# Finishing a modulation block: sums over partitions with the accumulator streamed, copied and turned

## The chip, the cores and the metric

The kernel runs on one core of a Trainium2 chip. The metric is device time in microseconds (us) of one execution; the time of a kernel is the median over its runs. TensorE (PE) multiplies; loading its stationary operand ("weights") is a separate instruction and is shown as PEld. VectorE is DVE, ScalarE is ACT, GpSimd is POOL; SP starts most of the DMA transfers. Each engine works through its own instructions in order.

## The reference, cut to what matters

```python
for layer in range(DEPTH):                                   # DEPTH = 2, D_MODEL = 1024
    mod_x = split(s_c  @ w_mod[layer] + b_mod[layer], 6)     # one row for the latent tokens
    mod_c = split(s_cc @ w_mod[layer] + b_mod[layer], 6)     # one row for the context tokens
    hx = modulate(rms_norm(x,   norm_mix_g[layer]), mod_x[0], mod_x[1])
    hc = modulate(rms_norm(ctx, norm_mix_g[layer]), mod_c[0], mod_c[1])
    ...                                                      # mixer of the layer
    x = x + mod_x[2] * ox
    fx = modulate(rms_norm(x, norm_ffn_g[layer]), mod_x[3], mod_x[4])
    x = x + mod_x[5] * conv_ffn(fx, ...)
```

`s_c` and `s_cc` are SiLU of the two conditioning vectors. `w_mod[layer]` is 1024 x 6144 in float32. Layer 0 has a Mamba-2 SSD mixer and RG-LRU blocks, layer 1 has HGRN2 and S5; each layer ends in a convolutional feed-forward network (FFN). There are 512 latent and 256 context tokens.

## The kernel before

Activations lie with channels on partitions, in a tile of 768 columns (256 context, 512 latent). A matmul of full precision is three matmuls of rounded parts: line 215 sends, for each slice of 128 input channels, `whi` with the high part, `whi` with the low part and `wlo` with the high part, for 512 latent columns (tile `px`) and for 256 context columns (tile `pc`). ACT rounds each weight panel to `whi`, DVE makes the rest `wlo`; four buffers of each are in turn.

The modulation matrix is cut into blocks of 256 output columns, named (layer l, block j), 24 to a layer. The first eight blocks of layer 0 are made at the start with matmuls (`mod_cols`, line 308: four groups of 32 weight columns side by side in the array, each with its own input rows, then a copy by ACT and two transposes, line 316). Block (0, 21) has a way of its own (`mod_now`). The other 39 blocks are spread over the kernel as ticks:

- `mod_tick` (line 347) handles one slice of 128 input channels of a block: a 128 x 256 piece of `w_mod` comes by DMA into `mst` (two buffers), and DVE adds piece times `sc` (the conditioning, one value to a partition) to the accumulator `macc`. For 23 blocks (15 of layer 0 and the first 8 of layer 1) there are two accumulators, latent and context (n = 2); for the last 16 blocks of layer 1 there is one (n = 1).
- After 8 ticks `macc` holds, on each partition, a partial sum for 256 outputs. `mod_pend` (line 367) puts the block on the list `PEND`; each call of `mtick` lets every pending block take one stage. Two empty stages (LAG = 2) come ahead of `finish` (line 369).
- `finish` adds up over the 128 partitions: for each half h and each accumulator e a matmul on line 373 with the 128 x 128 half of `macc` as weights and one column of ones streamed, into one column of the PSUM tile `pmodt`. Then two DVE operations (line 375) add the bias and write `MOD`.
- `macc()` (line 268) gives the next block one of two accumulator buffers, and forces the oldest pending block on while more than one would be held.
- PSUM tiles named `pmodt`, and many others (`pin`, `pst`, `pyi`, `pcbm`, `pyt`, `pnst`, ...), come from one ring of three banks (`pss`, line 92): a tile waits until the tile three before it in the ring has been read.

The order of instructions on each engine is not the order of the code: a list scheduler sets it when the kernel is built, so an added instruction can move its neighbours. In layer 0's mixer (about 215 to 585 us) the LRU phase and the SSD phase are woven together; in the output projection of layer 0 (about 585 to 705 us) matmuls on `rhi`/`rlo` are woven with the last SSD steps: `pin` (line 1111), `pst` (line 1099), `pyt` (line 1201). The FFN of layer 0 follows.

Of the kernel before, what the change touches and what calls it, by code (L numbers as in the profile page):

```python
# [9 lines left out]
F32 = mybir.dt.float32  # L10
# [28 lines left out]
PNS = {}  # L39
# [25 lines left out]
def build(tc, I, out, dbg=None):  # L65
# [26 lines left out]
    def pss(name="ps"):  # L92
        return pp.tile([128, 512], F32, tag="ps", name=name, bufs=3)
# [109 lines left out]
    def wpanel(W, r0, kt, c0, n, gain=None, byk=False, eng=None):  # L203
        return wsplit(wload(W, r0, kt, c0, n), kt, n, gain, byk, eng)
# [33 lines left out]
    def mod_advance(q):  # L238

        q["stages"].pop(0)()  # L240
        if not q["stages"]:
            PEND.remove(q)
# [24 lines left out]

    def macc():

        while len(PEND) + (TICK[0] % NQ > 0) > 1:  # L270
            mod_advance(PEND[0])
        return mp.tile([128, 2 if LIM[0] < len(MODSEQ) else 1, 256], F32, tag="macc", name="macc", bufs=2)

    def mod_row(ps, r):
        row = macc()[:, 0]
        V.tensor_copy(row[:r], ps[:r, :256])
        return row

    def mod_split(l, j, eng=None):

        w = wpanel(I["w_mod"][l], 0, 8, j * 256, 256, byk=True, eng=eng)
        ps = pss("pmod")
        for k in range(8):
            hi, lo = w[k // 4]
            PE.matmul(ps[:4, :256], sc4[:, k, :], hi[:, k % 4, :], start=(k == 0), stop=False)
            PE.matmul(ps[:4, :256], sc4[:, k, :], lo[:, k % 4, :], start=False, stop=(k == 7))
        row = mod_row(ps, 4)
        PEND.append({"l": l, "j": j, "stages": [lambda: mod_finish(l, j, row, 2, 2)]})

    def mod_now(l, j, st=None):  # L290

# [32 lines left out]
    NQ = 8  # L324
# [1 line left out]
    MST = []  # L326
    MACC = []

    PE_ = [j for j in range(8, 20) if (0, j) in MODP]

    def mod_pe(at):

        if at in PNS and PE_:
            k = PNS[at]
            (mod_now(0, PE_.pop(0)) if k == 1 else mod_split(0, PE_.pop(0), G if k == 2 else V))

    def mod_load():
        i = len(MST)
        if i < NQ * LIM[0]:
# [26 lines left out]

    def mod_pend(l, j, n, acc, lag):

        def finish():
            pt = pss("pmodt")  # L370
            for h_ in range(2):
                for e in range(n):
                    PE.matmul(pt[:, 2 * h_ + e:2 * h_ + e + 1], acc[:, e, h_ * 128:(h_ + 1) * 128], ones[:, 0:1], start=True, stop=True)  # L373
            for h_ in range(2):
                V.tensor_scalar(MOD[l][j // 4][:, j % 4 * 2 + h_, 0:n], pt[:, 2 * h_:2 * h_ + n], P("bm", l * 48 + j * 2 + h_), None, op0=ALU.add)
        PEND.append({"l": l, "j": j, "stages": [lambda: None] * lag + [finish]})

    def mod_vec(l, j, st):

# [167 lines left out]
    J0 = [(i % 2 == 0) * 4 + i // 2 for i in range(8)]  # L547
    xin, ST0 = [], {}
    sc = cp.tile([128, 8, 2], F32, name="sc")
    sc4 = cp.tile([128, 8, 4], F32R, name="sc4")  # L550
    sc32 = ldp.tile([128, 8, 32], F32, name="sc32")
    G.memset(sc32, 0.0)
    par0 = fetch_par(0, ldp, S)
# [5 lines left out]
    def mod0(i):  # L559
        if START[i] == 1:  # L560
            mod_cols(0, J0[i], ST0.pop(i))
        elif START[i] == 3:
            mod_vec(0, J0[i], ST0.pop(i))
        else:
            mod_split(0, J0[i], G if START[i] == 2 else V)

    def xturn(c):
        for hf in range(2):
# [18 lines left out]
    for c in range(6):  # L587
        xturn(c)
        if c == LP0:

            turn_par(*par0)
            act(sc[:, :, 0], PS("c", 0, 8), AF.Silu)
            act(sc[:, :, 1], PS("cc", 0, 8), AF.Silu)
            V.tensor_copy(sc32[:, :, 0:2], sc)
            V.tensor_copy(sc4[:, :, 0:2], sc)
            V.tensor_sub(sc4[:, :, 2:4], sc, sc4[:, :, 0:2].bitcast(F32))
        if c in M0C and m0 < n1:
            mod0(m0)
            m0 += 1
# [122 lines left out]
    def xbc_phase(xp):  # L722

        dtg = dt_phase(xp)

        XI = [0]

        def turn(b, t):
            q0, q1 = pss("ptx"), pss("ptc")
            tk = xp.tile([128, 6, 128], F32, tag="tk", name="tk")  # L730
            for c in range(6):
                d_ = q1[:, c * 128:(c + 1) * 128] if c < 2 else q0[:, (c - 2) * 128:(c - 1) * 128]
                PE.transpose(d_, t[:, c * 128:(c + 1) * 128], ident)
            act(tk[:, 0:2, :], q1[:, :256].rearrange("p (c x) -> p c x", x=128), AF.Copy)
            act(tk[:, 2:6, :], q0.rearrange("p (c x) -> p c x", x=128), AF.Copy)
            if b < 8:
                S.dma_start(xtok_d[:, :, b * 128:(b + 1) * 128].rearrange("c p x -> p c x"), tk)
            else:
                S.dma_start(btok_d[:, :, (b - 8) * 128:(b - 7) * 128].rearrange("c p x -> p c x"), tk)

        prev = None
        for pb in (4, 5, 0, 1, 2, 3):
            w = wx4 if pb == 4 else wpanel(W0, 0, 8, 1024 + pb * 256, 256, eng=G if KG[7] else V)
            blk = []
            if pb == 4:
                blk = [(psx(), psc()) for hf in range(2)]
                mm3g([(both(*blk[hf]), w, hf) for hf in range(2)], h, range(8))
            for hf in range(2):
                b = pb * 2 + hf
                if pb == 4:  # L750
                    px, pc = blk[hf]
                else:
                    px, pc = psx(), psc()
                    mm3(both(px, pc), w, hf, h, range(8))
                t = xp.tile([128, T], F32, tag="t768", name="xbct", bufs=3)
                conv1d(t, px, pc, lambda i: P("scw", i * 12 + b), P("scb", b), 4,
                       xp.tile([128, T], F32, tag="ctap", name="ctap", bufs=1) if b in CVP else None)
                act(t, t, AF.Silu)
                dump(f"xbc_{b}", t)
                if b >= 10:  # L760
                    S.dma_start(cch_d[b - 10], t)
                elif b >= 8:
                    S.dma_start(bch_d[b - 8], t)
                yield
                mod_pe(XI[0] // 2)
                mtick(MT[0] if XI[0] >= SSD0 - 4 else MT[4])
                XI[0] += 2
                if b == 8 or (b == 9 and next(dtg, None)):
                    pass
                if prev is not None:  # L770
                    turn(*prev)
                prev = (b, t) if b < 10 else None
                yield
            next(dtg, None)
        turn(*prev)
        for _ in dtg:
            pass
# [582 lines left out]
    with tc.tile_pool(name="lru", bufs=2, reuse_waits="tile") as lp:  # L1360

        acc = 0.0
        for at, _ in enumerate(lru_phase(lp)):
            mod_pe(12 + at)
            mtick(MT[1])
            acc += SSDR
            if acc >= 1.0:
                acc -= 1.0
                if ssd is not None and next(ssd) == "gate":
                    acc = -1e9  # L1370
        while acc > -1e8 and next(ssd) != "gate":
            pass
# [769 lines left out]
```

## Time and profile before

| what | value |
|---|---|
| runs | 2121.35 us median of 3 (2115.91 to 2133.28) |
| the profiled execution | 2126.28 us, span 2124.4 us, mean granted clock 0.968 |
| PE busy | 2011.8 us, 95% |
| DVE busy | 1568.3 us, 74% |
| ACT busy | 870.1 us, 41% |
| matmul records of line 373 | 248, two to each of 124 matmuls |
| mean granted clock, 215 to 700 us | 0.94 |
| mean granted clock, 700 to 1330 us | 1.00 |

A float32 matmul leaves two records (the 124 matmuls of line 373 leave 248), a transpose one. A timeline row merges records of one kind that follow each other: "x8" are eight records, the first number is the start of the first, the second the time they covered. A row's length is latency, and matmuls are pipelined: what a matmul costs a busy TensorE is the distance from its start to the start of the next. The granted clock is given as a share of full speed; it has two levels, 1.2 and 2.4 GHz.

### The profile page before, as it was taken

How to read it: one execution, taken by the hardware profiler on the slowest of the kernel's cores; microseconds unless marked ns; L12 is line 12 of the kernel's file. 1: busy time of each engine (PE TensorE's matmuls, PEld its weight loads, DVE VectorE, ACT ScalarE, POOL GpSimd, SP SyncE). 2: the span in 40 equal slices, each digit the busy share in tenths (PEclk: the TensorE clock that was granted, in tenths of full speed). 3: DMA queues.
4: the chain of work that ended last, by engine and by line, in shares of the span. 5: the costliest groups of instructions: out<-in, count | busy, mean ns of one | idle time of the engine just before them, and what ended most of it. 6: DMA issues, size and time to landing. Idle time of an engine off the chain costs nothing.

```text
span 2124.4 us, 32677 instructions
## 1 busy us (share of the span) xinstructions
PE 2011.8 (95%) x12738; PEld 1696.7 (80%) x12738; DVE 1568.3 (74%) x2934; ACT 870.1 (41%) x1267; POOL 259.8 (12%) x223
## 2 busy tenths in 40 slices
PE   7969989898898999999999999999999899999998
PEld 4758778787677888888888888987888688888887
DVE  5998898767778888867775665655877779668484
ACT  4725576586533442212321223424444344223234
POOL 2132333344421000000000000120001000000000
PEclk7979999999899999999999999999999999999999
DMA  9437435435676322333234212454422123322321
GB/s 334 133 104 207 152 98 169 128 97 162 222 245 218 100 85 97 110 119 119 90 112 134 82 47 98 130 155 149 136 80 68 41 80 99 100 88 92 99 85 55
DMA packets 283018, 261.09 MB, mean 123 GB/s; under 512 B 23405, under 2 KB 263060, under 8 KB 282864
## 3 DMA queue, kind: packets, MB, share of 16 engines
q1 hardware_dynamic: 257504, 243.35, 36.1%
q10 hardware_dynamic: 24464, 13.75, 2.3%
q8 instruction: 100, 1.64, 0.3%
q0 software_dynamic: 896, 1.90, 0.2%
q14 instruction: 54, 0.44, 0.1%
HBM read 224.17 MB, written 34.78 MB: 122 GB/s over the span
## 4 chain that ended last, share of the span: by engine, by line
PE 64%; DVE 5%; DMA 3%; issue 1%; ACT 1%; POOL 1%; SPq 0%; DVEq 0%; POOLq 0%; ACTq 0%
PE px L215 34%; PE pc L215 10%; PE pu L215 6%; PE pseg L215 4%; DMA mst<-in_w_mod_dram 1%; DVE macc L83 1%; PE pmodt L373 1%; PE pv L222 1%; PE pv L223 1%; PE pv L224 1%; PE pob L215 1%; PE plv L1886 1%; DVE qx L1937 0%; PE py L1735 0%; DMA st<-in_ev_w_out_dram 0%
## 5 line engine op out<-in xcount | busy, mean ns | idle before, releaser
L80 ACT ACTIVATE whi<-st 128x1024 fp32r<-128x1024 f32 (+1 forms) x197 | 203.5, 1037 | 581.0 <-PE pc L215 372.8
L215 PE MATMUL px<-HH,whi 128*128 128x512 f32 (+2 forms) x1016 | 408.6, 404 | 9.8 <-DVE u L83 4.7
L215 PE MATMUL px<-HL,whi 128*128 128x512 f32 (+2 forms) x1016 | 404.9, 399 | 0.9 <-DVE HL L83 0.9
L215 PE MATMUL px<-HH,wlo 128*128 128x512 f32 (+2 forms) x1016 | 404.7, 398 | 0.0
L193 DVE TENSOR_TENSOR wlo<-st,whi 128x1024 fp32r<-128x1024 f32 (+1 forms) x197 | 237.3, 1208 | 78.6 <-ACT whi L80 76.5
L83 DVE SCALAR_TENSOR_TENSOR macc<-mst,sc,macc 128x256 f32<-128x256 f32 x434 | 216.0, 528 | 70.5 <-DMA mst<-in_w_mod_dram 69.8
L83 DVE SCALAR_TENSOR_TENSOR fa<-px,par,fa 128x441 f32<-128x441 f32 (+2 forms) x352 | 241.8, 692 | 8.1 <-ACT fa L80 2.0
L215 PEld LDWEIGHTS px<-HH,whi 128*128 128x128 f32 (+1 forms) x1016 | 191.9, 189 | 55.3 <-DVE u L83 5.2
L215 PEld LDWEIGHTS px<-HL,whi 128*128 128x128 f32 (+1 forms) x1016 | 192.3, 189 | 45.2 <-DVE HL L83 1.9
L215 PEld LDWEIGHTS px<-HH,wlo 128*128 128x128 f32 (+1 forms) x1016 | 192.0, 189 | 44.4 <-issue 0.4
L215 PE MATMUL pc<-HH,whi 128*128 128x256 f32 (+1 forms) x728 | 207.4, 287 | 10.0 <-ACT ge L80 4.7
L215 PE MATMUL pc<-HH,wlo 128*128 128x256 f32 x728 | 206.8, 285 | 0.0
L215 PE MATMUL pc<-HL,whi 128*128 128x256 f32 (+1 forms) x728 | 206.8, 285 | 0.0
L215 PEld LDWEIGHTS pc<-HH,whi 128*128 128x128 f32 (+1 forms) x728 | 138.3, 190 | 14.4 <-ACT ge L80 5.5
L80 ACT ACT_TABLE_LOAD x105 | 134.7, 1283 | 11.4 <-DVE fa L83 3.6
L215 PEld LDWEIGHTS pc<-HL,whi 128*128 128x128 f32 (+1 forms) x728 | 138.4, 190 | 1.2
L215 PEld LDWEIGHTS pc<-HH,wlo 128*128 128x128 f32 x728 | 138.0, 190 | 0.6
L215 PE MATMUL px<-fhi,whi 128*128 128x512 f32 x304 | 120.6, 397 | 0.0
L215 PE MATMUL px<-flo,whi 128*128 128x512 f32 x304 | 120.0, 395 | 0.0
L215 PE MATMUL px<-fhi,wlo 128*128 128x512 f32 x304 | 119.8, 394 | 0.0
L1843 POOL TENSOR_TENSOR kc<-kc,e 128x255 f32<-128x255 f32 x6 | 6.5, 1082 | 847.0 <-ACT kc L80 674.8
L215 PE MATMUL pu<-HH,wlo 128*128 128x512 f32 (+1 forms) x192 | 74.3, 387 | 0.0
(655 smaller groups left out, 4260.2 us busy)
## 6 DMA issues: line engine op xcount, KB each, us to landing
mst<-in_w_mod_dram SPq DMA_DIRECT2D x312, 128.0 KB, 2.1
st<-in_ffn_w_gate_dram SPq DMA_DIRECT2D x22, 1024.0 KB, 4.9
st<-in_ffn_w_up_dram SPq DMA_DIRECT2D x22, 1024.0 KB, 5.0
st<-in_ev_w_in_dram SPq DMA_DIRECT2D x18, 1024.0 KB, 6.3
st<-in_ffn_w_down_dram SPq DMA_DIRECT2D x16, 1024.0 KB, 4.9
bc<-cum_d SPq DMA_DIRECT2D x24, 512.0 KB, 6.0
sth<-in_od_w_in_dram SPq DMA_DIRECT2D x24, 512.0 KB, 4.1
st<-in_w_mod_dram SPq DMA_DIRECT2D x9, 1024.0 KB, 11.2
```

What stands on the lines that cost most here:

```text
L80: return S.activation(o, i, f, bias=bias, scale=scale, **kw)
L83: return (eng or V).scalar_tensor_tensor(o, a, s, b, op0=op0, op1=op1)
L193: (eng or V).tensor_sub(lo, src, hi.bitcast(F32))
L215: PE.matmul(o, ww[:, k, :M], hh[k][part][:, sl], start=(first and q == 0 and a == 0), stop=(stop and q == last and a == 2))
L222: PE.matmul(o, hh[k][0][:, sl], whi[:, k % 4, :], start=(k == 0), stop=False)
L223: PE.matmul(o, hh[k][0][:, sl], wlo[:, k % 4, :], start=False, stop=False)
L224: PE.matmul(o, hh[k][1][:, sl], whi[:, k % 4, :], start=False, stop=(k == 7))
L373: PE.matmul(pt[:, 2 * h_ + e:2 * h_ + e + 1], acc[:, e, h_ * 128:(h_ + 1) * 128], ones[:, 0:1], start=True, stop=True)
L1843: G.tensor_mul(kc[:, 0, 0:255], kc[:, 0, 0:255], e0[:, 0:255])
L1886: PE.matmul(v3[r:r + 32, c, :], kk(j), qq(j), start=True, stop=True, tile_position=(0, r))
```

## The change

The ones become the weights and the accumulator is streamed. Each block's end is now two stages and not one. `sums`: for each of the 2n halves a matmul with 32 columns of ones as weights, in one of four column groups of the array (`tile_position=(0, q * 32)`), with 128 columns of `macc` streamed, so that every one of the 32 partitions of a group in the PSUM tile `pmods` holds the sums; then ACT copies the 128 x 128 (n = 2) or 64 x 128 (n = 1) tile to `mrow`, of which there is one buffer. `finish`: one transpose of `mrow` into `pmodt`, and the two DVE operations read one column of each group of 32. The stages are: one empty, `sums`, one empty, `finish`. A block no longer counts as holding an accumulator once its sums are taken. Code that is not run before is taken out (`mod_split`, `mod_pe`, two branches at the start), and with it two small DVE operations at the start that made `sc4`.

```diff
     def macc():
 
-        while len(PEND) + (TICK[0] % NQ > 0) > 1:
-            mod_advance(PEND[0])
+        while sum(q.get("acc", True) for q in PEND) + (TICK[0] % NQ > 0) > 1:
+            mod_advance([q for q in PEND if q.get("acc", True)][0])
...
     def mod_pend(l, j, n, acc, lag):
 
+        rows = 2 * n * 32
+        row = []
+
+        def sums():
+            ps = pss("pmods")
+            for q in range(2 * n):
+                PE.matmul(ps[q * 32:(q + 1) * 32, :128], ones[:, :32], acc[:, q % n, q // n * 128:(q // n + 1) * 128],
+                          start=True, stop=True, tile_position=(0, q * 32))
+            row.append(mp.tile([128, 128], F32, tag="mrow", name="mrow", bufs=1)[:rows])
+            act(row[0], ps[:rows, :128], AF.Copy)
+            pend["acc"] = False
+
         def finish():
             pt = pss("pmodt")
+            PE.transpose(pt[:, :rows], row[0], ident[:rows, :rows])
             for h_ in range(2):
-                for e in range(n):
-                    PE.matmul(pt[:, 2 * h_ + e:2 * h_ + e + 1], acc[:, e, h_ * 128:(h_ + 1) * 128], ones[:, 0:1], start=True, stop=True)
-            for h_ in range(2):
-                V.tensor_scalar(MOD[l][j // 4][:, j % 4 * 2 + h_, 0:n], pt[:, 2 * h_:2 * h_ + n], P("bm", l * 48 + j * 2 + h_), None, op0=ALU.add)
-        PEND.append({"l": l, "j": j, "stages": [lambda: None] * lag + [finish]})
+                V.tensor_scalar(MOD[l][j // 4][:, j % 4 * 2 + h_, 0:n], pt[:, h_ * n * 32:(h_ + 1) * n * 32:32],
+                                P("bm", l * 48 + j * 2 + h_), None, op0=ALU.add)
+        pend = {"l": l, "j": j, "acc": True, "stages": [lambda: None] * (lag - 1) + [sums, lambda: None, finish]}
+        PEND.append(pend)
...
@@ in the start-up
-            V.tensor_copy(sc4[:, :, 0:2], sc)
-            V.tensor_sub(sc4[:, :, 2:4], sc, sc4[:, :, 0:2].bitcast(F32))
```

How instructions stand on the engines is shown at two places. The first is TensorE in layer 0's FFN, at the end of an n = 2 block. Before:

```order
L215 MATMUL px<-HL,whi 128x512
L215 MATMUL pc<-HL,whi 128x256
L215 MATMUL px<-HH,wlo 128x512
L215 MATMUL pc<-HH,wlo 128x256
L373 MATMUL pmodt<-ones,macc 128x1 x4
L215 MATMUL px<-HH,whi 128x512
L215 MATMUL pc<-HH,whi 128x256
```

With the change (line numbers are those of the changed kernel: 364 is the transpose, 356 the sums):

```order
L215 MATMUL px<-HL,whi 128x512
L215 MATMUL pc<-HL,whi 128x256
L215 MATMUL px<-HH,wlo 128x512
L215 MATMUL pc<-HH,wlo 128x256
L364 MATMUL pmodt<-ident,mrow 128x128
L356 MATMUL pmods<-macc,ones 32x128 x4
L215 MATMUL px<-HH,whi 128x512
L215 MATMUL pc<-HH,whi 128x256
```

Four matmuls with 128 weight columns have given way to the transpose of one block and the four sums of the next, at the same seam between two weight panels; at other seams the transpose or the sums stand alone.

The second place is TensorE in the output projection of layer 0, where `pin`, `pst` and the block's tiles share the ring of three PSUM banks (in brackets: the engines or DMA queues that an instruction waits for). Before:

```order
L215 MATMUL pc<-rhi_5418,wlo 128x256
L373 MATMUL pmodt<-ones,macc 128x1 [waits DVE_49] x2
L373 MATMUL pmodt<-ones,macc 128x1 x2
L1111 MATMUL pin<-hs_5349,cch 128x512 [waits DMAHW2_49,DVE_49,Pool_49]
L1099 MATMUL pst<-xw,bt 128x512 [waits DMAHW5_49,DVE_49,Pool_49]
L1111 MATMUL pin<-hs_5350,cch 128x512 [waits DVE_49,DMAHW3_49,PE_49,Pool_49]
L1099 MATMUL pst<-xw,bt 128x512 [waits DMAHW6_49,DVE_49,Pool_49]
L215 MATMUL px<-rhi_5404,whi 128x512 [waits Activation_49]
```

With the change (1096 and 1084 are `pin` and `pst` there):

```order
L215 MATMUL pc<-rhi_5435,wlo 128x256
L364 MATMUL pmodt<-ident,mrow 128x128 [waits DVE_49]
L356 MATMUL pmods<-macc,ones 32x128 [waits DVE_49]
L356 MATMUL pmods<-macc,ones 32x128 x3
L1096 MATMUL pin<-hs_5366,cch 128x512 [waits DMAHW3_49,DVE_49,Pool_49]
L1084 MATMUL pst<-xw,bt 128x512 [waits DVE_49,DMAHW4_49,PE_49,Pool_49]
L1096 MATMUL pin<-hs_5367,cch 128x512 [waits DMAHW6_49,Activation_49,Pool_49]
L1084 MATMUL pst<-xw,bt 128x512 [waits DMAHW7_49,DVE_49,Pool_49]
```

There are now two tiles of the ring ahead of `pin`, `pst` and the second `pin`. The second `pin` gets the bank of `pmods` and waits for ACT (its copy to `mrow`), where before it got the bank of `pmodt` and waited for DVE; the first `pst` now gets the bank of `pmodt`. The 39 copies stand in ACT's order between the roundings of weight panels. DVE's accumulations stand within 18 instructions of where they stood.

## Rows read from the trace of the kernel before

**Rows 1.** The page: TensorE's busy line, and its chain by line.

```profile
PE 2011.8 (95%) x12738; PEld 1696.7 (80%) x12738; DVE 1568.3 (74%) x2934; ACT 870.1 (41%) x1267; POOL 259.8 (12%) x223
...
PE px L215 34%; PE pc L215 10%; PE pu L215 6%; PE pseg L215 4%; DMA mst<-in_w_mod_dram 1%; DVE macc L83 1%; PE pmodt L373 1%; PE pv L222 1%; PE pv L223 1%; PE pv L224 1%; PE pob L215 1%; PE plv L1886 1%; DVE qx L1937 0%; PE py L1735 0%; DMA st<-in_ev_w_out_dram 0%
```

**Rows 2.** By stretch: length; busy PE, PEld, DVE, ACT, POOL; granted clock; DMA share, GB/s.

```profile
215.00:700.00 485.00, 435.80 (x2522) 368.18 (x2521) 390.59 (x604) 293.22 (x422) 172.05 (x106) 0.94 0.52 164
700.00:1330.00 630.00, 628.46 (x3633) 549.67 (x3633) 449.86 (x870) 174.08 (x233) 0.00 (x0) 1.00 0.31 100
```

**Rows 3.** TensorE's timeline at an n = 2 block: start, us, what.

```profile
938.52 0.28 PE L215 MATMUL pc<-flo,whi 128*128 128x256 f32 x1
938.64 0.39 PE L215 MATMUL px<-fhi,wlo 128*128 128x512 f32 x1
938.87 0.28 PE L215 MATMUL pc<-fhi,wlo 128*128 128x256 f32 x1
938.98 0.95 PE L373 MATMUL pmodt<-ones,macc 128*128 128x1 f32 x8
...
940.12 0.28 PE L215 MATMUL pc<-fhi,whi 128*128 128x256 f32 x1
```

**Rows 4.** TensorE's timeline at an n = 1 block.

```profile
1078.05 0.28 PE L215 MATMUL pc<-HH,wlo 128*128 128x256 f32 x1
1078.17 0.50 PE L373 MATMUL pmodt<-ones,macc 128*128 128x1 f32 x4
...
1078.85 0.28 PE L215 MATMUL pc<-HH,whi 128*128 128x256 f32 x1
```

**Rows 5.** TensorE's timeline in HGRN2: matmuls in four column groups between others.

```profile
1556.47 0.28 PE L215 MATMUL pc<-HH,whi 128*128 128x256 f32 x1
1556.67 0.46 PE L1886 MATMUL plv<-qx,km 128*32 128x32 f32 x32
...
1557.40 0.28 PE L215 MATMUL pc<-HL,whi 128*128 128x256 f32 x1
```

**Rows 6.** Timeline of all engines in the output projection, around a `pmodt`.

```profile
611.11 1.10 PE L1111 MATMUL pin<-hs,cch 128*128 128x512 f32 x2
...
612.05 1.02 PE L1099 MATMUL pst<-xw,bt 128*128 128x512 f32 x2
...
613.57 1.67 DVE L83 SCALAR_TENSOR_TENSOR macc<-mst,sc,macc 128x256 f32<-128x256 f32 x4 [1.91 <-DMA mst<-in_w_mod_dram]
...
615.75 1.10 PE L1111 MATMUL pin<-hs,cch 128*128 128x512 f32 x2 [2.68 <-DVE mod L375]
```

**Rows 7.** TensorE's timeline at the start: line 308, also in four column groups.

```profile
47.26 0.28 PE L215 MATMUL pc<-HH,whi 128*128 128x256 f32 x1
47.47 1.07 PE L308 MATMUL pmod<-st,sc 128*32 128x256 f32 x16
48.47 0.44 PE L316 MATMUL pmodt<-ident,macc 128*128 128x128 f32 x2
```

**Rows 8.** TensorE's timeline near the end: two transposes between other matmuls.

```profile
2104.97 0.28 PE L215 MATMUL pseg<-fhi,whi 128*128 128x256 f32 x1
2105.20 0.44 PE L2091 MATMUL pfin<-ident,ft 128*128 128x128 f32 x2
2105.40 0.36 PE L215 MATMUL pseg<-flo,whi 128*128 128x256 f32 x1
2105.60 0.28 PE L215 MATMUL pseg<-fhi,wlo 128*128 128x256 f32 x1
```

**Rows 9.** ACT's groups by shape: busy, mean ns, idle before it.

```profile
L80 ACT ACTIVATE cb<-pcbm 128x128 f32<-128x128 f32 x12 | 3.3, 278 | 7.5 <-PE pcbm L1124 7.5
```

**Rows 10.** ACT's timeline in layer 0's FFN.

```profile
912.98 1.06 ACT L80 ACTIVATE whi<-st 128x1024 fp32r<-128x1024 f32 x1 [8.16 <-PE pc L215]
```

**Rows 11.** TensorE's waits: us in total, times, longest.

```profile
PE pin L1111 <- DVE mod L375: 6.6, 2, 3.9
```

**Rows 12.** Line 375 on DVE from 215 to 705 us: ns minimum, median, maximum.

```profile
L375 DVE TENSOR_SCALAR mod<-pmodt,par x22: 204/210/217, 217.2 to 701.6; 128x2 f32<-128x2 f32 x22
```

More of the change, by code (lines that the diff above doesn't have):

```diff
@@ L277, in mod_row @@
         return row
[L279 to L288, printed above, removed]
     def mod_now(l, j, st=None):
@@ L327, in build @@
     MACC = []
[L329 to L335, printed above, removed]
     def mod_load():
@@ L549, in build @@
     sc = cp.tile([128, 8, 2], F32, name="sc")
-    sc4 = cp.tile([128, 8, 4], F32R, name="sc4")
     sc32 = ldp.tile([128, 8, 32], F32, name="sc32")
@@ L561, in mod0 @@
             mod_cols(0, J0[i], ST0.pop(i))
[L562 to L565, printed above, removed]
     def xturn(c):
@@ L764, in xbc_phase @@
                 yield
-                mod_pe(XI[0] // 2)
                 mtick(MT[0] if XI[0] >= SSD0 - 4 else MT[4])
@@ L1363, in build @@
         for at, _ in enumerate(lru_phase(lp)):
-            mod_pe(12 + at)
             mtick(MT[1])
```

## The prediction

> **What bounds the kernel now.** I read the page first: TensorE is busy for 2011.8 of 2124.4 us, and the chain that ended last is mostly its line 215 [rows 1]. The same chain holds line 373, the matmuls that the change removes, with 1% of the span (rounded, so some 10 to 30 us): they are on the path. Next came the busy time by stretch. From 700 to 1330 us TensorE is busy for 628.46 of 630 us at a granted clock of 1.00, the 2.4 GHz level [rows 2]: there a matmul costs what it takes from TensorE, and whatever another engine does is hidden unless TensorE waits for it. From 215 to 700 us it is busy for 435.80 of 485, with DVE busy for 390.59 and ACT for 293.22, at a granted clock of 0.94 [rows 2]: there waits decide as well. Last I read the timeline around single blocks, for the price of the old sums and of everything that looks like the new ones.
>
> **What is removed.** The spacing of undisturbed matmuls is 0.12 us for 256 columns (938.52 to 938.64) and 0.23 us for 512 (938.64 to 938.87) [rows 3]. Around an n = 2 block the 256-column matmul at 938.87 and the one at 940.12 should be 0.12 + 0.23 = 0.35 apart, and are 1.25: the eight records cost 0.90 us, 0.11 each, the delay of the next 512-column matmul included [rows 3]. An n = 1 block costs 1078.85 - 1078.05 - 0.35 = 0.45 us, again 0.11 a record [rows 4]. One column is streamed, so this is the price of getting 128 weight columns into the array. With 23 blocks of the first kind and 16 of the second (23 x 4 + 16 x 2 = 124 matmuls) the change removes 20.7 + 7.2 = 27.9 us of TensorE's time. That is 1.3% of the run, and no more can be won on this way.
>
> A rule of the Trainium skill speaks against this: "TensorEngine Tiling (Array Packing)", section Performance Considerations, puts the overhead of a matmul at about 60 cycles, so that one column takes as long as sixty. By that the eight records would cost about 0.2 us, an estimate from that page, and the change would be a loss. The rows above measure 0.90, and the measurement decides; what remains of the idea is the fourth rival.
>
> **What is added to TensorE.** For `sums` 2n matmuls, two records each, in separate column groups, 128 columns each. The trace of before has the form at two other sizes. In HGRN2 32 records of 32 columns stand between two of line 215: from 1556.47 to 1557.40 is 0.93, less 0.35 leaves 0.58 us [rows 5]. Four groups run side by side, so these are 8 rounds. A 512-column float32 record costs 0.47 us (two from 611.11 to 612.05 [rows 6]), 32 columns 0.03, 8 rounds 0.24: the rest, 0.34 us, is the price of going into column groups and out again. At the start 16 records of 256 columns take 48.47 - 47.26 - 0.12 = 1.09 us [rows 7]; four rounds at 0.235 are 0.94, the rest 0.15, with only the way in fully counted. So the switch costs 0.15 to 0.34 us. I take 0.34, since there the neighbours are the ones that `sums` will have. `sums` has two rounds of 128 columns (0.12 each): 0.24 + 0.34 = 0.58 us, for n = 1 as for n = 2, since the groups lie side by side. At the low end it is 0.39.
>
> The transpose: two of them take 0.20 us from start to next start, and 2105.60 - 2104.97 - 0.24 = 0.39 with their seams [rows 8]. One costs between 0.10 and 0.20; I take 0.15.
>
> So a block costs 0.73 us (0.49 to 0.78). An n = 2 block gains 0.90 - 0.73 = 0.17 us, 3.9 over 23; an n = 1 block loses 0.73 - 0.45 = 0.28, 4.5 over 16. Sum: 0.6 us slower. With the low prices it is 23 x 0.41 - 16 x 0.04 = 8.8 us faster, with the high ones 23 x 0.12 - 16 x 0.33 = 2.5 us slower. About half of the blocks have the transpose of one directly ahead of the sums of the next, as in the first order shown, and share a seam; I give that 0.1 us each, 2 to 3 us in all. The net is 2 us faster, between 9 faster and 3 slower.
>
> **What is added elsewhere.** ACT gets 39 copies of a 128 x 128 PSUM tile, 0.278 us each by the nearest row (same shape, also from PSUM) [rows 9], 10.8 us together. In the FFN that is covered by ACT's own waiting: it stands idle for 8.16 us before a rounding [rows 10]. The copy stands beside that rounding, so it can delay a panel that is a panel ahead of its use by 0.3 us: nothing. In 215 to 700 us ACT is busy for 60%; if that cover were gone, 11 blocks x 0.278 = 3 us. DVE keeps its 78 small operations, now with a strided read; they are as many and as short, and the two that go at the start are of 16 elements per partition: nothing. The accumulator is free one stage earlier, which lets DVE start the next but one block sooner; with TensorE at 628.46 of 630 us that is worth nothing in the FFN. `MOD` is written one stage later; the code forces pending stages where a value is needed, and then the copy by ACT stands in line between sums and transpose, 0.3 us each at a handful of places.
>
> **The ring of three PSUM banks.** Here a stall goes and another comes. Before, the second `pin` of a step in the output projection takes the bank of `pmodt` and waits until DVE has written `MOD`; DVE is late because the next block's accumulations stand ahead and wait for their DMA (1.91 us, then 1.67 of work), and TensorE loses 2.68 us [rows 6]. That happened twice, 6.6 us in all [rows 11]. Afterwards that `pin` waits for ACT's copy, and the first `pst` stands behind DVE's operation. Queued behind either on TensorE is the rest of the projection. I count one wait for one wait: nothing, with bounds of 6.6 us gained (none waits) and 36 us lost (second rival below).
>
> **Sum.** 2 us faster. The profiled execution took 2126.28 us (span 2124.4 and 1.9 around it), 4.9 us above the median of the runs, which spread by 17 us; so the profile would show about 2124, and the median goes from 2121.35 to 2119 us. That is the forecast: no change that can be seen. I call faster or slower what is over 1%, 21 us, about what a measurement of this kernel can tell from no change.
>
> **The rivals.**
>
> *Column groups cost no switch.* Then a block costs 0.24 + 0.15 = 0.39, and the change gains 23 x 0.51 + 16 x 0.06 = 12.7 us: 2109 us. For it: the 0.15 of [rows 7]. Against it: the 0.34 of [rows 5], in the kind of place where most sums will stand. The same page of the Trainium skill gives up to four times the throughput for 32 columns (Theoretical Speedup), which is this case, but also says that changing the tiling mode drains the engine (Key Properties); the 0.34 is such a price.
>
> *The ring makes waits (the other side).* Each block now takes two banks, one freed by ACT and one by DVE. Eleven blocks end before 705 us (22 bias operations, two to a block [rows 12]). If each lost what a wait of before lost, 6.6 / 2 = 3.3 us [rows 11], that is 36 us: 2155 us. It decides from seven waits on (23 us). For it: DVE is busy for 390.59 of 485 us there [rows 2] and its queue has accumulations waiting for DMA [rows 6], ACT's queue has roundings. Against it: before, two of eleven blocks waited, and the wait that the change puts in the place of the old one is for an engine with 40% of its time free.
>
> *The new order closes gaps.* The list scheduler places everything from 215 to 700 us anew, and 485 - 435.80 = 49 us of TensorE's time are idle there [rows 2]. If half were closed, 25 us: 2094 to 2097 us. For it: the waits there are short and each belongs to the order. Against it: nothing in the change aims at them, and DVE, which is nearly as busy, does the same work as before.
>
> *The weight loads were hidden anyway.* Were the removed matmuls free, the change would cost 39 x 0.73 = 28 us: 2150 us. Only the skill's rule speaks for it; the 0.90 and 0.45 of [rows 3, 4] speak against it.
>
> **How the numbers follow.** The forecast gets 0.61, with its own range 2110 to 2129 (the bounds of 9 faster and 3 slower, and some us for the runs). No switch 0.07, waits in the ring 0.16 (0.12 of it beyond 1%), closed gaps 0.14 (0.10 of it beyond 1%), hidden weight loads 0.02. With 0.01 on either side for the forecast's own tail: faster 0.11, slower 0.15, within 1% 0.74. The range goes from 2099 to 2146: it leaves out the far part of the closed gaps (0.08) and of the waits, with the hidden loads (0.10).
>
> **What would show it.** In the FFN the matmul behind a transpose and sums should stand 0.6 to 0.8 us later than undisturbed, for n = 1 as for n = 2; 0.4 would be the first rival. TensorE's busy share from 700 to 1330 us should stay at nearly all. In the output projection the wait of `pin` for line 375 should be gone and one for `mrow` or for the bias operation should stand there; more than 25 us of such waits would be the second rival, and an idle time of TensorE from 215 to 700 us that has fallen by 20 us the third. The prediction is wrong if the median leaves 2099 to 2146.

## The result, and the profile after

The changed kernel takes 2143.22 us (median of 5 runs, 2140.57 to 2150.76); the kernel before, on the same chip, 2124.18 us. The ratio is 1.0103, 95% interval 1.0081 to 1.0124 (it is not the quotient of the medians): about 1% slower, 19 us by the medians and 22 by the ratio. The forecast was 2119, no change. The profiled execution has a span of 2138.6 us, 14.2 more than before, at the same mean clock of 0.968.

The busy times and the chain that ended last, from the page of the changed kernel; they answer to [rows 1]:

```profile
PE 2011.4 (94%) x12777; PEld 1678.3 (78%) x12777; DVE 1567.6 (73%) x2932; ACT 880.3 (41%) x1308; POOL 258.6 (12%) x223
...
PE 71%; DVE 14%; DMA 7%; ACT 4%; issue 2%; POOL 2%; SPq 0%; ACTq 0%; DVEq 0%; POOLq 0%
```

The same chain in the kernel before:

```profile
PE 64%; DVE 5%; DMA 3%; issue 1%; ACT 1%; POOL 1%; SPq 0%; DVEq 0%; POOLq 0%; ACTq 0%
```

TensorE is as busy as before (2011.8), ACT by 10.2 us more. The span is longer, so TensorE waits more: DVE's share of the chain rose from 5 to 14%. Busy time by stretch of the changed kernel, which answers to [rows 2]:

```profile
215.00:700.00 485.00, 426.65 (x2469) 354.44 (x2469) 378.42 (x581) 294.30 (x420) 167.91 (x105) 0.93 0.51 161
700.00:1330.00 630.00, 628.34 (x3646) 539.52 (x3644) 446.86 (x869) 171.60 (x251) 0.00 (x0) 0.99 0.31 99
```

From 215 to 700 us TensorE is idle for 58.35 us (49.20 before). The FFN's stretch is as full as before.

To see where the 14.2 us come from, I number in both traces the matmuls into `px`, `pc`, `pz`, `pseg` and `pu` (9000 in each, by start) and subtract the start of the k-th before from that of the k-th after. Where the two orders differ, the k-th is not the same matmul in both, so the number then says how far ahead or behind the work is by count. The columns are the time of that matmul in the kernel before, each row is one profiled execution; the last column is the difference of the medians over the runs, for comparison:

| us later than before, at | 176 | 535 | 581 | 728 | 756 | 1054 | 1295 | 1327 | 2110 | medians |
|---|---|---|---|---|---|---|---|---|---|---|
| changed kernel | -3.3 | -12.1 | +7.5 | +5.7 | +10.8 | +7.3 | +10.6 | +11.8 | +14.2 | +19.0 |
| e1_first4_old | -5.1 | +3.7 | +1.3 | +0.1 | +5.1 | +1.7 | +5.0 | +7.2 | +10.6 | +10.7 |
| e2_old_ops_lag3 | -0.3 | -4.1 | +11.1 | +13.5 | +13.6 | +12.8 | +12.7 | +12.7 | +13.6 | +11.4 |
| e3_first11_new | +0.2 | -6.0 | +13.9 | +13.2 | +15.5 | +14.7 | +14.5 | +14.6 | +17.0 | +10.4 |
| e4_n2_ffn_new | -5.9 | +0.8 | +0.1 | -1.2 | -1.1 | -4.6 | -4.8 | -4.8 | -3.3 | -3.1 |
| e5_first4_old_early_stage | -3.9 | +2.1 | -0.1 | -1.3 | -1.0 | -3.7 | -1.2 | +2.2 | +5.9 | +4.6 |
| e6_all_new_weave_025 | -6.1 | -4.9 | -11.8 | -14.0 | -4.9 | -8.4 | -5.1 | -2.9 | +0.4 | +9.9 |
| e7_before_weave_025 | -0.4 | +15.3 | +9.4 | +15.4 | +15.4 | +15.4 | +15.4 | +16.9 | +19.2 | +10.6 |
| e8_n2_from_fifth_early_stage | -2.1 | +4.0 | +1.6 | +0.8 | +1.0 | -2.5 | -2.7 | -2.7 | -1.9 | -1.7 |
| e9_first3_old_early_stage | -1.3 | -5.7 | +16.7 | +21.3 | +21.4 | +18.7 | +21.3 | +23.3 | +26.5 | +22.5 |
| e10_first4_old_n1_128rows | -0.8 | +4.3 | +2.1 | +1.6 | +1.8 | -1.0 | +0.1 | +1.6 | +5.1 | +3.7 |

Where the last two columns differ by 4 us or more (the changed kernel itself by 4.8, e3, e6, e7 and e9 by 4 to 10), the profiled execution was not a typical one, and the sizes of single steps are good to some us only; where a step lies is read from it. The column 176 is the spread of the start. In the kernels that keep the order of before up to 581 us (e1, e4, e5, e8, e10) a lead there is gone by 581, where they stand within 2.1 us of before. Five steps make up the changed kernel's 14.2 us: 7.5 up to 581 (the mixer; 10.8 if the lead of 3.3 at 176 is counted, which the old order would have lost as well), -1.8 from there to 728, 5.1 from 728 to 756 (the entry of layer 0's FFN), -3.5 to 1054 (blocks with n = 2), and +6.9 from there to the end (the stretch of the blocks with n = 1).

**The mixer.** `pcbm`, `pin`, `pst` and `pyi` are matmuls of an SSD step; the z matmuls (into `pz`) are placed between the steps and fill their waits. TensorE from the last z matmul (it starts at 534.32 us) to the output projection, changed kernel; a choice of the matmuls of the SSD and the first of the projection, with the wait ahead of each in brackets:

```profile
534.44 0.38 PE L1109 MATMUL pcbm<-cch,bch 128*128 128x128 f32 x2
...
543.95 3.65 PE L1135 MATMUL pyi<-xt,bc 128*128 128x64 f32 x16 [7.41 <-issue]
547.39 0.74 PE L1109 MATMUL pcbm<-cch,bch 128*128 128x128 f32 x2
...
550.48 1.89 PE L1135 MATMUL pyi<-xt,bc 128*128 128x64 f32 x16
...
555.03 2.43 PE L1135 MATMUL pyi<-xt,bc 128*128 128x64 f32 x16 [1.26 <-DVE bc L1123]
559.25 4.19 PE L1084 MATMUL pst<-xw,bt 128*128 128x512 f32 x4 [1.79 <-POOL xw L1077]
568.34 0.79 PE L215 MATMUL px<-rhi,whi 128*128 128x512 f32 x1 [4.90 <-ACT rhi L80]
...
577.53 1.02 PE L1096 MATMUL pin<-hs,cch 128*128 128x512 f32 x2
578.39 1.02 PE L1084 MATMUL pst<-xw,bt 128*128 128x512 f32 x2
...
581.05 3.62 PE L287 MATMUL pmod<-st,sc 128*2 128x256 f32 x16
```

The same place in the kernel before, where the last z matmul starts at 546.32:

```profile
552.18 3.65 PE L1150 MATMUL pyi<-xt,bc 128*128 128x64 f32 x16 [5.59 <-issue]
555.62 3.73 PE L1099 MATMUL pst<-xw,bt 128*128 128x512 f32 x4
559.14 1.30 PE L1111 MATMUL pin<-hs,cch 128*128 128x512 f32 x2
560.28 1.02 PE L1099 MATMUL pst<-xw,bt 128*128 128x512 f32 x2
...
563.34 3.62 PE L298 MATMUL pmod<-st,sc 128*2 128x256 f32 x16
566.89 0.50 PE L215 MATMUL px<-rhi,whi 128*128 128x512 f32 x1
```

In the new order the z matmuls ran ahead (the -12.1 at 535), and three SSD steps (three `pyi`) are left for the end, not one. There each step waits for the one before it through DVE, POOL and ACT, with no other matmul to fill in. Busy time in that gap, changed kernel (stretch, its length, then PE, PEld, DVE, ACT and POOL, the granted clock, DMA share and GB/s):

```profile
534.60:568.30 33.70, 18.02 (x66) 10.99 (x65) 25.14 (x30) 10.65 (x14) 18.20 (x12) 0.72 0.57 183
```

and in the gap of the kernel before:

```profile
546.60:566.90 20.30, 14.56 (x45) 7.56 (x45) 12.05 (x17) 8.18 (x11) 10.55 (x9) 0.75 0.74 252
```

TensorE is idle for 15.7 us of the gap, not 5.7. And the work that filled the gap before (`pmod` and two pairs of `pin` and `pst`) now stands behind it, inside the projection: the projection's matmuls shift from -0.2 to +6.9 where it stands (577.53 to 584.60 us).

**The FFN's entry** and **the prices** are shown with the experiments that settle them.

### The profile page after: what moved, and what is told of

Same layout as the page of the kernel before. It is cut to its first block, busy times and chain, and to the rows that moved or that the text cites. A ratio compares the mean times of both kernels' runs of the same rounds, so it can differ in the third digit from the quotient of the medians.

```text
span 2138.6 us, 32841 instructions
## 1 busy us (share of the span) xinstructions
PE 2011.4 (94%) x12777; PEld 1678.3 (78%) x12777; DVE 1567.6 (73%) x2932; ACT 880.3 (41%) x1308; POOL 258.6 (12%) x223
## 3 DMA queue, kind: packets, MB, share of 16 engines
q8 instruction: 100, 1.64, 0.3%
## 4 chain that ended last, share of the span: by engine, by line
PE 71%; DVE 14%; DMA 7%; ACT 4%; issue 2%; POOL 2%; SPq 0%; ACTq 0%; DVEq 0%; POOLq 0%
PE px L215 37%; PE pc L215 12%; PE pu L215 6%; PE pseg L215 4%; DMA mst<-in_w_mod_dram 2%; DVE macc L83 2%; DVE wlo L193 1%; ACT L80 1%; ACT gate L80 1%; DVE xbct L83 1%; DMA xin<-in_x_dram 1%; DVE bc L1116 1%; DVE gate L1312 1%; DVE u L83 1%; PE pz L223 1%
## 5 line engine op out<-in xcount | busy, mean ns | idle before, releaser
L80 ACT ACT_TABLE_LOAD x107 | 137.3, 1283 | 11.1 <-DVE fa L83 3.8
L215 PE MATMUL pu<-HL,whi 128*128 128x512 f32 (+1 forms) x192 | 74.4, 388 | 0.0
```

The lines of the kernel that those rows point to most:

```text
L80: return S.activation(o, i, f, bias=bias, scale=scale, **kw)
L215: PE.matmul(o, ww[:, k, :M], hh[k][part][:, sl], start=(first and q == 0 and a == 0), stop=(stop and q == last and a == 2))
```

## Experiments

Theory A: the loss is the new order in the mixer. Theory B: it is the price of the new operations, their banks and ACT's copy. Where an experiment has the old finish, it is the code of before, kept beside the new in the changed kernel. In expectations "the jump of 19.6 us" is the step from -12.1 to +7.5 above.

**One: the first four blocks old.**

```diff
-            mod_pend(l, j, n, acc, LAG)
+            (mod_pend if i // NQ >= 4 else mod_pend_old)(l, j, n, acc, LAG)
```

> The first four blocks of the 39 (those that end between 215 and 370 us) keep the old finish; the other 35 have sums, copy and transpose. Built this way, TensorE's order at the end of layer 0's mixer is that of the kernel before: one pyi is left behind the last z matmul, not three. Theory A (the loss is the new order of the SSD steps in the woven mixer, not a price of the new operations): within 5 us of the kernel before, ratio 0.997 to 1.003, and no jump of 19.6 us between 530 and 595 us. Theory B (the loss is the price of the new operations, their waits for banks and for ACT's copy): 35 of 39 blocks bear it, so at least 12 us slower, ratio above 1.006. The step of 4.9 us at the entry of layer 0's FFN (735 to 763 us) should be there if it belongs to the new operations, and be gone if it came with the late arrival from the mixer.

Measured 2137.96 us, ratio 1.005 (1.003 to 1.007). The jump is gone (+3.7 at 535, +1.3 at 581), as theory A says, though 35 blocks have the new finish. But the total is not within 5 us of before: the step at the FFN's entry stays at 5.0 us, and from 1054 us on it loses another 8.9. So the order is only part of the loss.

**Two: no new operation, one more empty stage.** All 39 blocks have the old finish, and `LAG` is 3 where before it was 2.

> The kernel before in every operation (all 39 blocks with the old finish); only one more empty stage ahead of each finish (three, not two). Built this way the order in the mixer falls so that three pyi, one pcbm, two pin and two pst are left behind the last z matmul, nearly as in the changed kernel. Theory A (order): 8 to 20 us slower than before, ratio 1.004 to 1.010, lost between 530 and 600 us, although not one new operation is in it. Theory B (price of the new operations): the same as before, ratio 0.999 to 1.001.

Measured 2138.64 us, 1.005 (1.0033 to 1.0067). Theory A's band: 11.4 us are lost up to 581 us without one new operation, 2.4 more to 728 us and nothing after (+13.5 at 728, +13.6 at the end). Waits of TensorE from 535 to 600 us in it:

```profile
PE px L215 <- ACT rhi L80: 5.3, 1, 5.3
PE pst L1096 <- POOL xw L1089: 2.6, 2, 2.0
PE pz L222 <- ACT zt L80: 2.0, 1, 2.0
PE pyi L1147 <- DVE bc L1135: 1.5, 1, 1.5
```

They are the waits of the changed kernel's gap (for `rhi`, `xw` and `bc`) over again.

**Three: only the first 11 blocks new** (`i // NQ < 11`).

> Only the first 11 blocks (those that end before 705 us) have the new finish, the other 28 the old one. The order at the end of the mixer is that of the changed kernel (three pyi left over). Theory A: 12 to 20 us slower than before, ratio 1.006 to 1.010, as the whole change. Theory B, if the loss is spread over the blocks: 11 of 39 of 19 us, 5 us slower, ratio 1.0025.

Measured 2137.64 us, 1.0052 (1.0031 to 1.0073): 10.4 us by the medians; in the profiled execution (17.0) 13.7 are lost up to 581 us. Where the loss lies is as theory A says, and theory B's even spread (5 us) is too small; the size by the medians lies below A's 12 to 20.

**Four: only the 12 blocks with n = 2 in the FFN new** (`i // NQ >= 11 and n == 2`).

> The new finish only for the 12 blocks with two accumulators that end in layer 0's FFN after 705 us; the first 11 and the 16 with one accumulator keep the old one. Up to 705 us the order is that of the kernel before. By the slope seen in the changed kernel's FFN (about 0.25 us gained per block of this kind) theory A expects 3 us faster than before, ratio 0.998 to 1.000; by the prediction's price (0.17 each) 2 us. Theory B: 12 of 39 of 19 us, 6 us slower, ratio 1.003.

Measured 2124.12 us against 2127.23, ratio 0.9985 (0.9971 to 0.9999): 3.1 us faster, by theory A. In the table it stands at -1.1 at 756 and at -4.6 at 1054 us, 3.5 us for these 12 blocks. Its interval ends just below 1, the only one here that does; experiment eight's overlaps it.

**Five: as one, with the transpose at the stage of the old finish.**

```diff
-        ... "stages": [lambda: None] * (lag - 1) + [sums, lambda: None, finish]}
+        ... "stages": [lambda: None] * (lag - 2) + [sums, lambda: None, finish]}
```

> As the kernel in which the first four blocks keep the old finish, but with the one empty stage ahead of the sums left out, so that the transpose stands at the stage at which the old finish stood. That kernel lost 4.8 us at the entry of layer 0's FFN (735 to 763 us): there the last two blocks whose values the FFN's norm needs were finished right ahead of the norm's sums (pnst), and the second transpose waited 1.34 us on TensorE. Theory C (the loss at the entry is the one stage more, and the copy by ACT in that chain): the step at 735 to 763 us is at most 1 us, and the whole is 5 to 7 us slower than before, ratio 1.0025 to 1.0035, down from 1.005. Rival (the loss at the entry is another order of the norm's own instructions): the step stays at 4 to 5 us, ratio 1.005.

Measured 2130.26 us, 1.0024 (1.0013 to 1.0036), just below what was expected. The step from 728 to 756 us fell from 5.0 to 0.3: theory C. The FFN's entry in experiment one, TensorE and one copy by ACT; the two `pmodt` are the last two blocks that this FFN's norm needs, `pmods` is the sums of the second of them:

```profile
709.11 0.42 PE L356 MATMUL pmods<-macc,ones 128*32 128x128 f32 x8
734.85 0.27 PE L364 MATMUL pmodt<-ident,mrow 128*128 128x128 f32 x1
737.21 0.26 ACT L80 ACTIVATE mrow<-pmods 128x128 f32<-128x128 f32 x1
737.52 0.33 PE L364 MATMUL pmodt<-ident,mrow 128*128 128x128 f32 x1 [1.34 <-DVE mod L366]
737.68 1.85 PE L445 MATMUL pnst<-ones,xsq 128*128 128x1 f32 x16
...
749.69 0.50 PE L215 MATMUL px<-HH,whi 128*128 128x512 f32 x1 [1.65 <-ACT HH L80]
```

and in experiment five:

```profile
733.43 0.27 PE L364 MATMUL pmodt<-ident,mrow 128*128 128x128 f32 x1
733.54 1.84 PE L445 MATMUL pnst<-ones,xsq 128*128 128x1 f32 x16
```

In experiment one both blocks' last stage comes only at the norm, over 25 us after the last sums; the second transpose waits 1.34 us, the norm's sums (`pnst`) stand behind it, and the first matmul of the FFN waits 1.65 us for the normed input. The second transpose has to follow the second block's copy, and `mrow` has one buffer, which the first block holds until its transpose at 734.85: the copy, of sums taken at 709.11, runs only at 737.21. It ends at 737.47, together with the first block's bias operations (`mod`), which the trace names. A second buffer was not tried. In the kernel before the last bias operations of these blocks start at 710.54 us, and TensorE waits for nothing from there to 770 us. The two waits are 3.0 us; most of the other 2.0 is the clock: busy time and granted clock (third figure from the end) from 748 to 762 us in experiment one:

```profile
748.00:762.00 14.00, 12.36 (x51) 10.05 (x51) 12.89 (x26) 6.87 (x11) 0.00 (x0) 0.88 0.50 160
```

and in experiment five:

```profile
748.00:762.00 14.00, 14.00 (x68) 11.56 (x68) 12.14 (x27) 5.25 (x10) 0.00 (x0) 1.00 0.25 80
```

After the wait matmuls of 512 columns stand 0.43 us apart for some us, not 0.23. The changed kernel has the same wait of the FFN's first matmul (1.64 us at 755.38) and the same 0.88, from 753.7 to 767.7 us. Its second transpose shows no such wait, but the granted clock is low ahead of the FFN as well: 0.76 from 741 to 748 us, behind the transposes and `pnst`, and 0.76 from 755 to 762. By an estimate from these shares each stretch costs 7 x 0.24 = 1.7 us; with the wait that is 5.0 of the 5.1 us.

**Six and seven: another weave.** `SSDR`, the rate at which SSD steps are drawn into the LRU phase, from 0.15 to 0.25, in the changed kernel and in the kernel before.

> The whole change, but the SSD steps are drawn into the woven mixer at a rate of 0.25 and not 0.15 per step of the LRU. Built this way no pyi is left behind the last z matmul (three are in the changed kernel). Theory A (19 us of the loss are the SSD steps left over at the end of the mixer): the jump of 19.6 us between 530 and 595 us goes; since the changed kernel stood 8 to 12 us ahead before that jump, the sum comes to between 5 us slower and 5 us faster than before, ratio 0.9975 to 1.0025. Theory B (new operations in the mixer): the jump stays, ratio 1.008 to 1.010.

> Control for the weave: the kernel before with the same rate of 0.25. One pyi is left behind the last z matmul, as before. Theory A: within 6 us of the kernel before, ratio 0.997 to 1.003, since the tail keeps its form; if the rate itself moved time by more than that, the run with the whole change at this rate has to be read against this one.

Measured 2135.55 us (1.0042, 1.0028 to 1.0057) and 2136.23 us (1.0057, 1.0035 to 1.0079) against 2125.66. Both miss their bands against the kernel before: the rate alone costs 10.6 us, although the tail keeps its one `pyi`, so the number of steps left over is not the whole of what an order is worth. Against its own control the whole change costs nothing (0.7 us faster by the medians, well inside the intervals), where at the rate of 0.15 it cost 19. That fits theory A; theory B alone does not give it, though the pair settles nothing by itself, since the two orders differ here too (no `pyi` is left over in six, one in seven), and a better order could hide a price. The profiled executions of the two lie 7.6 us below and 9.1 us above their medians, so nothing smaller is read from their traces.

**Eight: what gains, put together.** Experiment five with the condition `i // NQ >= 4 and n == 2`.

> The new finish for the 19 blocks with two accumulators from the fifth on, with the transpose at the old finish's stage; the first four blocks and the 16 with one accumulator keep the old finish. It joins what the runs so far say gains and leaves out what loses. Theory A with 0.25 us gained per block: 19 x 0.25 = 4.8 us faster than before, less up to 1 us at the FFN's entry: 3.8 to 4.8 us, ratio 0.9977 to 0.9982. By the prediction's price of 0.17: 3.2 us, 0.9985. If the copies and banks of the seven blocks ahead of 705 us cost waits: 1.000 or slower.

Measured 2124.00 us, 0.9998 (0.9986 to 1.0011): less than the 3.8 to 4.8 us expected. The seven blocks more, which end ahead of 705 us, bring nothing that shows; whether waits of theirs eat the gain is open. In the table the FFN's blocks gain as in experiment four (3.5 us from 756 to 1054). Five and eight differ in the 16 blocks with n = 1 alone: 2130.26 - 2124.00 = 6.3 us, 0.39 a block, all that these blocks bring about included.

**Nine: one block more than in five** (`i // NQ >= 3`).

> As the kernel with the first four blocks old and the early stage (ratio 1.0024), with one single block more given the new finish: the fourth, which ends near 367 us. Built this way the order at the end of the mixer tips over: three pyi, one pcbm, two pin and two pst are left behind the last z matmul, not one pyi. Theory A (order): 8 to 18 us slower than that kernel, ratio 1.006 to 1.011, with the jump of over 10 us back between 535 and 600 us; the two kernels differ in a single block. Theory B (price of new operations): one block more is at most 0.5 us, ratio 1.0024 to 1.003.

Measured 2145.86 us, 1.0102 (1.0082 to 1.0121), against 1.0024: the finish of one block, whose price differs by some 0.2 us, moves the time by over 16 us. Its profiled execution loses 18.0 us from 176 to 581 us (experiment five: 3.8), and its end of the mixer again has the serial waits:

```profile
545.28 2.40 PE L1147 MATMUL pyi<-xt,bc 128*128 128x64 f32 x10 [2.00 <-DVE bc L1135]
...
567.17 2.08 PE L1096 MATMUL pst<-xw,bt 128*128 128x512 f32 x2 [4.50 <-POOL xw L1089]
...
577.46 0.80 PE L215 MATMUL px<-rhi,whi 128*128 128x512 f32 x1 [5.84 <-ACT rhi L80]
```

**Ten: n = 1 with 128 rows.** Experiment five, where a block with n = 1 fills all four groups, each half twice.

```diff
-        rows = 2 * n * 32
+        rows = 128
...
-            for q in range(2 * n):
+            for q in range(4):
```

> As the kernel with the first four blocks old and the early stage (ratio 1.0024), but the blocks with one accumulator fill all four column groups (each half twice) and turn 128 rows, not 64. Theory D (the transpose of 64 rows is dear because it is another tile of the array: 0.40 us alone against 0.11 for 128 rows in the FFN): a transpose of such a block alone costs 0.11, sums stay at 0.53 to 0.55 since the groups lie side by side, a joint seam costs 0.66 and not 0.74; 16 blocks gain 16 x 0.15 to 0.29, 2 to 4 us: ratio 1.0005 to 1.0015. If the 0.40 is the price of this place and not of the 64 rows: 0.40 stays and the ratio is 1.0024 or above.

Measured 2127.10 us, 1.0008 (0.9991 to 1.0024). That lies 3.7 us above its own kernel before by the medians, where five lay 4.6 above its own; the ratios (1.0008 and 1.0024) differ by 3 us, and their intervals overlap. So the totals don't separate the two; the seams do. A transpose of an n = 1 block in the changed kernel, 64 rows:

```profile
1102.89 0.39 PE L215 MATMUL px<-HH,wlo 128*128 128x512 f32 x1
1103.12 0.28 PE L215 MATMUL pc<-HH,wlo 128*128 128x256 f32 x1
1103.33 0.27 PE L364 MATMUL pmodt<-ident,mrow 64*128 64x64 f32 x1
1103.53 0.50 PE L215 MATMUL px<-fhi,whi 128*128 128x512 f32 x1
1103.87 0.28 PE L215 MATMUL pc<-fhi,whi 128*128 128x256 f32 x1
```

From `pc` to `pc` it is 0.75 where 0.35 is the undisturbed distance: 0.40 us. One in experiment ten, 128 rows:

```profile
1129.37 0.28 PE L215 MATMUL pc<-fhi,wlo 128*128 128x256 f32 x1
1129.49 0.27 PE L364 MATMUL pmodt<-ident,mrow 128*128 128x128 f32 x1
...
1129.84 0.28 PE L215 MATMUL pc<-fhi,whi 128*128 128x256 f32 x1
```

That is 0.47, so 0.12 us; the four transposes of n = 1 blocks that stand alone from 1050 to 1300 us cost 0.11 each by unrounded times. So theory D holds: the smaller transpose is the dearer one.

**Eleven: sums twice**, in experiment four: `for q in list(range(2 * n)) * 2`.

> As the kernel with the new finish for the 12 blocks of two accumulators in the FFN alone, with each block's sums sent twice (the second time over the first, so nothing in the result changes). It measures the switch into and out of column groups by itself: the 8 records cost 0.55 us at an undisturbed seam; 8 more in the same groups are two more rounds of 128 columns. If streaming is 0.24 and the switch 0.31, 16 records cost 0.79. If the groups don't run side by side, 8 more records cost 8 x 0.12 = 0.94: 1.49. If there is no switch and a round costs 0.27: 1.10.

One run, for its trace. Sums of an n = 2 block alone, changed kernel:

```profile
956.44 0.28 PE L215 MATMUL pc<-fhi,wlo 128*128 128x256 f32 x1
956.65 0.43 PE L356 MATMUL pmods<-macc,ones 128*32 128x128 f32 x8
957.01 0.50 PE L215 MATMUL px<-fhi,whi 128*128 128x512 f32 x1
957.34 0.28 PE L215 MATMUL pc<-fhi,whi 128*128 128x256 f32 x1
```

and with 16 records, experiment eleven:

```profile
944.76 0.28 PE L215 MATMUL pc<-fhi,wlo 128*128 128x256 f32 x1
944.97 0.65 PE L356 MATMUL pmods<-macc,ones 128*32 128x128 f32 x16
945.55 0.50 PE L215 MATMUL px<-fhi,whi 128*128 128x512 f32 x1
945.88 0.28 PE L215 MATMUL pc<-fhi,whi 128*128 128x256 f32 x1
```

957.34 - 956.44 - 0.35 = 0.55 and 945.88 - 944.76 - 0.35 = 0.77. Eight records more cost 0.22 us, so four groups do run side by side, and 0.55 - 0.22 = 0.33 us is left for the switch into and out of column groups.

## Why the prediction was wrong, point by point

**Removed: right.** The rows' 0.90 and 0.45 us are what the change frees: experiment four's 3.1 to 3.5 us over 12 blocks are about what they leave over the new price (12 x 0.24 = 2.9).

**Added, n = 2: right.** 0.73 was worked out for sums and transpose. At undisturbed seams of the FFN the sums alone cost 0.55, the transpose alone 0.11 and both together 0.66: 0.24 gained per block, not 0.17. The 0.34 for the switch, taken from [rows 5], measured 0.33. "TensorEngine Tiling (Array Packing)" of the Trainium skill, Key Properties, has a change of tiling mode drain the engine, without a price. The trace agrees that there is one, 0.33 us. The switch-free rival (0.39 a block) fell. The 0.1 us that the sum gave back for a shared seam is not there for these blocks: 0.66 is 0.55 and 0.11.

**Added, n = 1: mis-sized.** The prediction gave these blocks the transpose of an n = 2 block, 0.15. With 64 rows it costs 0.40 alone, 0.21 beside sums (0.74 together). So a block costs 0.74 (shared seam) to 0.93 and loses 0.29 to 0.48, not 0.28; 0.39 by experiments five and eight. The two kinds together: 23 x 0.24 = 5.5 gained, 16 x 0.39 = 6.2 lost, 1 us slower where the sum had 0.6 slower and, with shared seams, 2 faster. This term hardly matters to the verdict.

**ACT's copies: right as a sum.** 39 copies of 0.260 us (median); ACT's busy time rose by 10.2 us, with 10.8 forecast.

**`MOD` one stage later: the first step that failed.** The prediction put "0.3 us each at a handful of places". In the changed kernel it cost 5.1 us at one place. What was missed is how long the next stage takes to come: where no call of `mtick` falls between the sums and the norm that needs the value, the last stages are forced there, on TensorE ahead of the norm's own sums, and with one `mrow` the second block's copy stands behind the first block's transpose. Then the FFN's first matmul waited 1.64 us, and the granted clock was 0.76 in two stretches of 7 us, one ahead of that wait and one behind it. Experiment five shows it: with the transpose a stage earlier the step is 0.3 us.

**The ring: right.** The wait of `pin` for the bias operation (6.6 us, 2 times [rows 11]) is gone; `pst` waits for it instead, once. Waits of TensorE from 585 to 712 us, changed kernel:

```profile
PE pst L1084 <- DVE mod L366: 3.5, 1, 3.5
PE pin L1096 <- POOL hs L1089: 1.2, 1, 1.2
```

One wait for one wait, as counted; the rival with waits in the ring at eleven blocks fell, and from 581 to 728 us the changed kernel even gains 1.8 us.

**The new order: the step that failed most.** The prediction knew that everything from 215 to 700 us is placed anew, but reckoned with that only as a rival that closes gaps (2094 to 2097 us), and put nothing in the sum for an order that opens them. It cost 7.5 of the 14.2 us in the profiled execution (10.8 with the lead at the start); by the medians, 8.3 us lie between the changed kernel and experiment one, which keeps the old order there. The old trace could not give its size; that there was such a term could be seen: the order of the changed kernel was there to be read, and in it three `pyi` stood behind the last z matmul where there had been one. I compared the orders only at the seams that the sum priced. Experiment two, which has no new operation, shows that order alone does this, and three and nine agree; why the scheduler's choice tips over with one block's finish or one empty stage, no run shows.

The rest of the loss by the medians (19 us) against the profiled spans (14.2 us) is the spread of executions. From 1295 to 1327 us the changed kernel loses 1.2 us and experiment five, with new n = 1 blocks too, 3.4. The first matmul of layer 1's mixer waits there for its normed input, 2.1 and 2.3 us, but in the kernel before 1.5 us are waited at that place as well (two waits); in experiment five the granted clock from 1295 to 1331 us is 0.91 where before it is 1.00, and 36 x 0.09 = 3.2 us is most of its step, by an estimate from these shares. So some of the 0.39 a block may be this and not the price of the operations. What is late there was not tried.

**What would have shown it**: the delay of 0.6 to 0.8 us per transpose with sums was there, TensorE stayed full from 700 to 1330 us, `pin`'s wait was gone. The third sign, idle time from 215 to 700 us, moved, but up by 9 us.

## What to carry to other kernels

Where a list scheduler places the instructions, an edit of 0.2 us can move a woven stretch by 10 to 20 us. Here every kernel with another order in the mixer lost (six of them, 9.9 to 22.5 us by the medians, other steps included). Compare the two orders along the whole stretch, above all what is left for its end once the filling work has run out, and give the order a term of its own in the sum; to judge the edit itself, hold the order fixed (leave the blocks that tip it as they were) or measure against a control with another order. When a step is put a stage later, find the place where its result is needed first and count the ticks left before it, and look at what holds a single buffer until then.

## What the runs showed of the hardware

- A transpose with 64 rows (64x64 out) costs a busy TensorE 0.40 us between matmuls of the full array, one with 128 rows 0.11; filling the rows with copies of the data was the cheaper way (experiment ten). The Trainium skill, "TensorEngine Tiling (Array Packing)", Tiling Modes, lists 64-row tiles among the modes. By that this would be the same kind of switch as the sums' 0.33; that it is one was not tried apart.
- Float32 matmuls of 32 weight columns in four column groups run side by side: eight records of 128 columns cost 0.22 us more, 0.03 a record, on top of 0.33 us that are left for the switch (experiment eleven).
- Where the stream had been gapless (granted clock 1.00 from 748 to 762 us in the kernel before), the granted clock was 0.88 behind waits of 1.34 and 1.65 us, with matmuls of 512 columns at 0.43 us each, at the 1.2 GHz level, and not 0.23: 3.0 us of waiting came to a step of 5.0 us (experiment one). In the changed kernel it was 0.76 from 741 to 748 us as well, behind two transposes and sixteen records of one column, with no wait listed there; why is open.
